# Near-key attention scores: three fp32r matmuls with split operands, or one fp32 matmul per 64x32 tile

## The chip, the cores and the metric

One core of a Trainium2 chip runs the whole program. The metric is device time in microseconds (us) of one execution, lower is better. All data are fp32 in memory; "fp32r" is the type under which TensorE reads an fp32 word at reduced precision in one pass, and "fp32" the type under which one matmul stands in the trace as two records of the same shape, two passes.

## What is computed

Two layers of a decoder, for a prompt of 1024 tokens and a sample group of 32 tokens. Layer 0 projects the normalised input to seven parts, runs a causal depthwise convolution of width 31 on one branch and attention on the other, and projects both back. Layer 1 is a gated linear recurrence. The change lies in the attention of the prompt in layer 0. There are 16 heads of width 64, and each query sees three sets of keys:

```python
DSWA_CONFIGS = ((128, 1), (512, 4), (2048, 16))   # (window, dilation)
scores = einsum('ndbqhe,ndbkhe->ndbhqk', qb, kk) * (hd ** -0.5)   # per config, by stride
lse = logsumexp(scores, axis=-1)
o = einsum('ndbhqk,ndbkhe->ndbqhe', exp(scores - lse), vv)
...
w = softmax(lses, axis=0)                          # merge of the three configs
yb = einsum('cnth,cnthe->nthe', w, outs)
```

The kernel folds the three sets into one softmax: a key that is in m of the sets has weight m, which a mask adds to the score. A query needs all keys of its own and the previous 128-token block ("near"), and further back only those at a distance that is a multiple of 4 ("far").

## The kernel before

**Work of layer 0.** Feature rows are on the 128 partitions, tokens along the free axis. Every projection is a "dense" job: 128 output features, three token chunks of 384, 384 and 288 (`CW`), and for each chunk 24 fp32r matmuls (8 slices of the contraction, three products of high and low parts each) into one PSUM tile (`d`, or `x` where a bank is spare). For head pair 0 to 7 the jobs are `ag`, `av` (the convolution's gate and value), `v`, `k`, `q`; then come the 8 `g` and the 8 `ao` jobs (gates), then the output projection. When the last `av` chunk of pair p is done, `conv_thread` (L1215) is spawned: 26 taps on DVE as multiply-adds of 128x1024, 5 taps as ACT products added on POOL, a join, and a store to DRAM (`yd`). When the last `q` chunk is done, `attention` (L995) is spawned. After the attention of a pair `dec_thread` (L1432) does the sample group, with 16 loads of cached keys and values (`kc`, `vc`) for each pair.

**Rotation.** `ev_q` and `ev_k` (L843, L866) evacuate a chunk of q or k: `rope` (L813) multiplies by cosines on DVE, swaps halves on ACT, multiplies by sines on POOL and adds on DVE. q is written in class order (`by_class`): in each block of 128 tokens the 32 tokens with position = r mod 4 stand together, for r = 0 to 3. Two more steps follow in the chain of every chunk, `hi` and `lo`: `hi` writes the fp32r copy of each head's half on ACT (2 casts of 64 partitions for q, 4 for k), and `lo` the difference to the fp32 value on DVE (2 subtractions of 64 partitions). `st` holds q's high part of a head in that head's 64 partitions and its low part in the other 64; `kk` holds k's high part in both halves; `kl` holds k's low part. These are 5 pages of 1056 columns beside `q` and `k`.

**Attention of a block.** `qk(i)` (L1003) makes the scores of block i (128 queries, two heads). Near keys: `nn` = 256 columns (128 for block 0), as two matmuls per head, `st` with `kk` over all 128 partitions (high and low part of q times high part of k at once), and then q's high part with `kl` over 64 partitions. Far keys: `nf` = 32 i columns for i of 2 or more, in fp32, as 8 tiles of 64 rows by 32 columns of the array, one per class r and head h; the keys of class r are read with a stride of 4 (`r:128 * i:4`). Then DVE adds the mask and takes the row minimum (`tensor_tensor_reduce`, shown as CUSTOM_DVE_ANT_0), and ACT takes the exponential. `tr(i)` (L1038) transposes the near part in blocks of 128 on TensorE, `far(i)` (L1055) the far part in blocks of 128 or 64 columns (`FAR`: (first block, end, group, width)), DVE or ACT copies the transposes to SBUF, and `pv(i)` and `far_pv` multiply by the values.

**What sets the order.** Every engine's order is written at build time by a planner (`Kern`, L177) that keeps a clock for each engine and models every instruction's cost (`array`, L239, for TensorE; `cost`, L266, for the others). Dense matmuls are laid down in a fixed order; between them `sides` (L402) places steps of the threads (Atoms) whose inputs are ready by the model, by priority: the rotation 0, the v transposes 1, attention 2, decode 3, the convolution 5. A DVE step is placed only while DVE's clock is less than 800 ns (`QUEUE`) ahead of TensorE's. A step of attention on TensorE needs inputs that were ready 300 ns ago by the model (`LEAD`). Buffers are pages of SBUF: a job or thread starts when the pages that it claims are free (`claim`; 28 pages in all). The planner's idea of a tile's time is one line of `array`:

```python
one = max(0.4167 * n + 5 if fast else 0.8333 * n + 5, ld)
```

Of the kernel before, what the change touches and what calls it, by code (L numbers as in the profile page):

```python
# [176 lines left out]
class Kern:  # L177
# [61 lines left out]
    def array(self, s, name, a, k):  # L239
# [11 lines left out]
        if mode == (128, 128):  # L251
            d = max(0.4375 * n + 8, 107) if fast else 109 if name == "transpose" else 2 * max(0.8333 * n + 4, 111)
            free, f = s + d, s + d + 165
        else:
            p = k.get("tile_position") or (a[1].base_partition() if hasattr(a[1], "base_partition") else 0,
                                            a[0].base_partition() if hasattr(a[0], "base_partition") else 0)
            s = max(s, self.tiles.get(p, 0.0))
            ld = m / 1.2 + 20
            one = max(0.4167 * n + 5 if fast else 0.8333 * n + 5, ld)
            r = 1 if fast else 2  # L260
            self.tiles[p] = s + r * one
            free, f = s + 7 * r, s + ld + r * one + 165
# [580 lines left out]
    def ev_q(self, pr, c, p):  # L843
        nc, A = self.nc, self.A
        S = self.pair[pr]
        w = CW[c]
        if c == 0:
            S["st"] = (A.alloc(T, True), A.alloc(T, True))
            S["q"] = A.alloc(NTOK)
        cs = slice(C0[c], min(C0[c] + w, T))  # L850
        half = [(slice(64 * h, 64 * h + 64), slice(64 - 64 * h, 128 - 64 * h)) for h in range(2)]
        q = S["q"]

        def hi():
            for h, (a, b) in enumerate(half):
                nc.scalar.copy(S["st"][h].r[a, cs], q[a, cs])

        def lo():
            for h, (a, b) in enumerate(half):
                nc.vector.tensor_tensor(S["st"][h].r[b, cs], q[a, cs], S["st"][h][a, cs], op=OP.subtract)  # L860
            if c == 2:
                nc.gpsimd.tensor_copy(self.qs[:, pr * NS:pr * NS + NS], q[:, T:NTOK])

        self.rope(p, c, "rq", pr, q, [Atom(hi, "act"), Atom(lo, "dve")])

    def ev_k(self, pr, c, p):  # L866
        nc, A = self.nc, self.A
        S = self.pair[pr]
        w = CW[c]
        if c == 0:  # L870
            S["kk"] = (A.alloc(T, True), A.alloc(T, True))
            S["kl"] = A.alloc(T, True)
            S["k"] = A.alloc(NTOK)
        cs = slice(C0[c], min(C0[c] + w, T))
        half = [(slice(64 * h, 64 * h + 64), slice(64 - 64 * h, 128 - 64 * h)) for h in range(2)]
        k = S["k"]

        def hi():
            for h, (a, b) in enumerate(half):
                nc.scalar.copy(S["kk"][h].r[a, cs], k[a, cs])  # L880
            for h, (a, b) in enumerate(half):
                nc.scalar.copy(S["kk"][h].r[b, cs], S["kk"][h][a, cs])

        def lo():
            for h, (a, b) in enumerate(half):
                nc.vector.tensor_tensor(S["kl"].r[a, cs], k[a, cs], S["kk"][h][a, cs], op=OP.subtract)
            if c == 2:
                nc.gpsimd.tensor_copy(self.ks[:, pr * NS:pr * NS + NS], k[:, T:NTOK])

        self.rope(p, c, "rk", pr, k, [Atom(hi, "act"), Atom(lo, "dve")])  # L890
# [104 lines left out]
    def attention(self, pr):  # L995
# [7 lines left out]
        def qk(i):  # L1003
            def f():
# [5 lines left out]
                qc, kc = slice(128 * i, 128 * i + 128), slice(128 * (i + 1) - nn, 128 * (i + 1))  # L1010
                hs = [slice(64 * h, 64 * h + 64) for h in range(2)]
                ss = []
                for h in range(2):
                    P[i, h] = A.alloc(W + 8)
                    ss.append(self.px())
                    nc.tensor.matmul(ss[h][:, nf:W], S["st"][h].r[:, qc], S["kk"][h].r[:, kc], start=True, stop=False)
                for h in range(2):
                    nc.tensor.matmul(ss[h][:, nf:W], S["st"][h].r[hs[h], qc], S["kl"].r[hs[h], kc],
                                     start=False, stop=True)
                if nf:  # L1020
                    for r in range(4):
                        for h in range(2):
                            nc.tensor.matmul(ss[h][32 * r:32 * r + 32, 0:nf],
                                             S["q"][hs[h], 128 * i + 32 * r:128 * i + 32 * r + 32],
                                             S["k"][hs[h], r:128 * i:4], start=True, stop=True,
                                             skip_group_check=True, tile_position=(64 * h, 32 * r))
# [28 lines left out]
        def far(i):  # L1055
            def f():
                p = self.px()
                parts = [n for n, (t0, t1, g, m) in enumerate(FAR) if t0 <= i < t1]
                for n, x in enumerate(parts):
                    g, m = FAR[x][2:]  # L1060
                    for h in range(2):
                        a = 256 * n + 128 * h
                        nc.tensor.transpose(p[0:m, a:a + 128], P[i, h][:, 128 * g:128 * g + m], self.ident)
# [68 lines left out]
        def fin1():  # L1132
# [8 lines left out]
            for n in ("st", "kk"):  # L1141
                for b in S[n]:
                    b.free()
            for n in ("q", "k", "kl", "vt", "vf"):
                S[n].free()
# [1193 lines left out]
    def plan_jobs(self):  # L2339
# [17 lines left out]
        for p in range(NPAIR):  # L2357
            J["v", p] = job("v", 5, p, self.ev_v, 1, 0)
            J["g", p] = job("g", 6, p, self.ev_g, 1, 1, self.gate_thread)
            J["k", p] = job("k", 4, p, self.ev_k, 4, 4)  # L2360
            J["q", p] = job("q", 3, p, self.ev_q, 3, 4, self.attention)
# [292 lines left out]
```

## Time and profile before

| | |
|---|---|
| time, median of 3 runs | 2397.56 us (2393.16 to 2400.98) |
| the profiled execution's own time | 2401.23 us, of which the instructions span 2399.4 us |
| busy, of the span | PE 95%, DVE 71%, ACT 46%, POOL 44% |
| granted TensorE clock, mean | 0.984 of 2.4 GHz |
| chain of waits that ended last | PE 70%, DVE 18%, ACT 3%, issue 3%, DMA 3%, POOL 2% |
| moved by DMA | 271.52 MB, mean 113 GB/s |

The profile is one execution. "Busy" of TensorE (PE) is the union of its matmuls' intervals; matmuls are pipelined, so their mean durations are longer than the distance between them. PEld is the loading of the stationary operand, which runs beside PE. Tiles are called by their pools: `d`, `x` and `o` are PSUM tiles, `b` and `c` SBUF buffers. A form such as 64*32 64x224 is 64 rows by 32 columns of the array with 224 columns streamed. The helper through which all engines are called makes L157 the line of every instruction, so forms and tiles tell them apart. In order of time: layer 0's jobs with attention up to about 750 us, decode attention and the gate jobs to about 1100, the output projection to about 1300, and layer 1 after that.

### The profile page before, as it was taken

What the parts mean: (1) busy time and instruction counts of PE and PEld (TensorE: products, weight loads), DVE (VectorE), ACT (ScalarE), POOL (GpSimd) and SP (SyncE); (2) the same over time, 40 slices, a digit from 0 to 9 for tenths busy, and PEclk for the clock granted to TensorE, in tenths of its full rate; (3) what the DMA queues carried; (4) which work ended last, traced back from release to release, by engine and by line L of the source; (5) the groups of instructions that cost most, each with busy time, mean ns of one, the idle gap of its engine ahead of it and who ended that gap; (6) DMA issues with size and microseconds to landing.
All of it is one profiled execution on the core that took longest, in us unless ns stands there. A gap on an engine that the chain in (4) does not pass through costs nothing.

```text
span 2399.4 us, 41471 instructions
## 1 busy us (share of the span) xinstructions
PE 2277.0 (95%) x16619; PEld 2141.0 (89%) x16619; DVE 1700.2 (71%) x2567; ACT 1094.7 (46%) x2000; POOL 1047.6 (44%) x700
## 2 busy tenths in 40 slices
PE   7989999989999999999988999999999999999997
PEld 7977977978879877889988999999999999998996
DVE  7999989999998766654486666656666666667336
ACT  5554554544645343334345444444444444444432
POOL 6653743634645253344464333333323333335436
PEclk9999999999999999999999999999999999999998
DMA  4221221221222798875351111211111112232525
GB/s 152 62 72 41 72 70 29 83 76 39 74 83 98 256 348 334 310 282 179 107 188 61 64 63 64 69 68 63 63 66 63 64 63 73 76 108 92 180 99 174
DMA packets 118169, 271.52 MB, mean 113 GB/s; under 512 B 32336, under 2 KB 59472, under 8 KB 117968
## 3 DMA queue, kind: packets, MB, share of 16 engines
q1 hardware_dynamic: 117968, 268.78, 32.7%
q8 instruction: 133, 2.18, 0.4%
q14 instruction: 68, 0.56, 0.1%
HBM read 215.00 MB, written 53.73 MB: 112 GB/s over the span
## 4 chain that ended last, share of the span: by engine, by line
PE 70%; DVE 18%; ACT 3%; issue 3%; DMA 3%; POOL 2%; SPq 0%; DVEq 0%; ACTq 0%; POOLq 0%
PE d L157 41%; PE x L157 29%; DVE b L157 18%; ACT b L157 3%; POOL b L157 2%; DMA b<-vc 1%; PE o L157 1%; DVE c L157 1%; DMA b<-x 1%; DMA b<-kc 0%; DMA ybd<-b 0%; DMA b<-rd 0%; SPq L157 0%; DMA b<-x1d 0%; DMA cpo<-b 0%
## 5 line engine op out<-in xcount | busy, mean ns | idle before, releaser
L157 PE MATMUL d<-c,b 128*128 128x384 f32 (+1 forms) x8064 | 1410.7, 330 | 18.3 <-ACT b L157 7.8
L157 PEld LDWEIGHTS d<-c,b 128*128 128x128 f32 x8064 | 1317.7, 190 | 49.8 <-issue 23.1
L157 POOL TENSOR_TENSOR b<-b,b 128x1024 f32<-128x1024 f32 (+8 forms) x418 | 834.2, 2007 | 833.7 <-ACT b L157 600.7
L157 ACT ACTIVATE b<-b 128x384 f32<-128x384 f32 (+14 forms) x647 | 357.9, 568 | 802.6 <-DVE b L157 788.5
L157 PE MATMUL x<-c,b 128*128 128x384 f32 (+4 forms) x3472 | 560.1, 311 | 30.1 <-DVE b L157 16.3
L157 PEld LDWEIGHTS x<-c,b 128*128 128x128 f32 (+2 forms) x3472 | 514.0, 174 | 57.8 <-ACT b L157 22.5
L157 DVE TENSOR_TENSOR b<-b,b 128x384 f32<-128x384 f32 (+15 forms) x397 | 405.4, 1033 | 93.3 <-ACT b L157 74.3
L157 DVE SCALAR_TENSOR_TENSOR b<-b,c,b 128x1024 f32<-128x1024 f32 (+2 forms) x258 | 387.5, 1505 | 10.9 <-ACT b L157 8.4
L157 ACT CAST b<-b 128x1024 fp32r<-128x1024 f32 (+5 forms) x408 | 293.1, 727 | 44.8 <-DVE b L157 11.4
L157 PE MATMUL x<-b,b 128*32 128x128 f32 (+11 forms) x3760 | 295.7, 329 | 6.2 <-POOL b L157 2.3
L157 DVE SCALAR_TENSOR_TENSOR b<-b,b 128x384 f32<-128x384 f32 (+3 forms) x216 | 201.5, 937 | 104.8 <-ACT b L157 104.1
L157 PEld LDWEIGHTS x<-b,b 128*32 128x32 f32 (+2 forms) x3760 | 218.6, 138 | 55.4 <-issue 27.2
L157 DVE TENSOR_TENSOR b<-d,b 128x384 f32<-128x384 f32 (+3 forms) x283 | 142.7, 511 | 147.7 <-PE d L157 140.4
L157 DVE TENSOR_TENSOR b<-x,b 128x288 f32<-128x288 f32 (+3 forms) x157 | 79.6, 507 | 127.9 <-PE x L157 112.9
L157 POOL TENSOR_SCALAR b<-b 128x32 f32<-128x32 f32 x40 | 28.8, 720 | 295.5 <-DVE b L157 295.4
L157 ACT COPY b<-x 128x512 f32<-128x512 f32 (+5 forms) x177 | 88.2, 514 | 137.6 <-PE x L157 129.8
L157 ACT COPY b<-d 32x384 f32<-32x384 f32 (+2 forms) x210 | 94.2, 448 | 106.7 <-DVE b L157 58.7
L157 DVE COPY b<-x 128x512 f32<-128x512 f32 (+6 forms) x214 | 96.0, 463 | 59.9 <-PE x L157 53.6
L157 POOL COPY b<-b 128x32 f32<-128x32 f32 (+2 forms) x105 | 56.4, 546 | 152.4 <-DVE b L157 150.2
L157 ACT ACTIVATE b<-b,c 128x512 f32<-128x512 f32 (+1 forms) x112 | 94.8, 875 | 3.0 <-DVE b L157 0.5
L157 DVE CUSTOM_DVE_ANT_0 b<-x,b 128x256 f32<-128x256 f32 (+8 forms) x144 | 71.8, 534 | 22.2 <-PE x L157 21.6
L157 PE MATMUL o<-b,b 128*64 128x128 f32 (+1 forms) x864 | 59.7, 269 | 27.4 <-DVE b L157 26.1
(59 smaller groups left out, 954.7 us busy)
## 6 DMA issues: line engine op xcount, KB each, us to landing
b<-wc SPq DMA_DIRECT2D x64, 512.0 KB, 3.8
b<-wab SPq DMA_DIRECT2D x56, 512.0 KB, 5.7
b<-kc SPq DMA_DIRECT2D x64, 448.0 KB, 6.4
b<-vc SPq DMA_DIRECT2D x64, 448.0 KB, 8.5
b<-woa SPq DMA_DIRECT2D x32, 512.0 KB, 4.6
b<-woc SPq DMA_DIRECT2D x32, 512.0 KB, 3.8
b<-yd SPq DMA_DIRECT2D x16, 528.0 KB, 8.8
ybd<-b SPq DMA_DIRECT2D x16, 512.0 KB, 3.2
```

The source lines that it names most:

```text
L157: r = f(*a, **k)
```

## The change

The near scores are no longer three products of split operands. They are computed like the far ones: fp32 `q` and `k` straight from the rotation, 8 tiles of 64x32, the near keys with unit stride, and the far keys right behind them in the same tiles. With that `hi` and `lo` go, with the pages of `st`, `kk` and `kl`: 144 casts on ACT and 96 subtractions on DVE. The far transposes always take 128 columns; of the blocks that took 64, the other 64 rows of the PSUM tile are written and not read. The planner gets a factor `u` of 2 for tiles of 64 rows that have another number of columns. The jobs `k` and `q` claim 1 page where they claimed 4 and 3.

```diff
@@ array
             ld = m / 1.2 + 20
-            one = max(0.4167 * n + 5 if fast else 0.8333 * n + 5, ld)
+            u = 2 if mode[0] == 64 != mode[1] else 1
+            one = max(0.4167 * n * u + 5 if fast else 0.8333 * n * u + 5, ld)
@@ ev_q, ev_k
-            S["st"] = (A.alloc(T, True), A.alloc(T, True))
...
-                nc.scalar.copy(S["st"][h].r[a, cs], q[a, cs])
...
-                nc.vector.tensor_tensor(S["st"][h].r[b, cs], q[a, cs], S["st"][h][a, cs], op=OP.subtract)
...
-        self.rope(p, c, "rq", pr, q, [Atom(hi, "act"), Atom(lo, "dve")])
...
+    def ev_turned(self, pr, c, p, n, smp):
         S = self.pair[pr]
         if c == 0:
+            S[n] = self.A.alloc(NTOK)
+        t = S[n]
+
+        def copy():
+            self.nc.gpsimd.tensor_copy(smp[:, pr * NS:pr * NS + NS], t[:, T:NTOK])
+
+        self.rope(p, c, "r" + n, pr, t, [Atom(copy, "pool")] if c == 2 else [])
@@ attention, qk(i)
-                    nc.tensor.matmul(ss[h][:, nf:W], S["st"][h].r[:, qc], S["kk"][h].r[:, kc], start=True, stop=False)
-                for h in range(2):
-                    nc.tensor.matmul(ss[h][:, nf:W], S["st"][h].r[hs[h], qc], S["kl"].r[hs[h], kc],
-                                     start=False, stop=True)
-                if nf:
+                q, k = S["q"], S["k"]
+                for a, b, ks in ((nf, W, kc), (0, nf, None)):
                     for r in range(4):
                         for h in range(2):
...
+                            if b > a:
+                                nc.tensor.matmul(ss[h][32 * r:32 * r + 32, a:b],
+                                                 q[hs[h], 128 * i + 32 * r:128 * i + 32 * r + 32],
+                                                 k[hs[h], ks or slice(r, 128 * i, 4)], start=True, stop=True,
+                                                 skip_group_check=True, tile_position=(64 * h, 32 * r))
@@ attention, far(i)
-                        nc.tensor.transpose(p[0:m, a:a + 128], P[i, h][:, 128 * g:128 * g + m], self.ident)
+                        nc.tensor.transpose(p[:, a:a + 128], P[i, h][:, 128 * g:128 * g + 128], self.ident)
@@ plan_jobs
-            J["k", p] = job("k", 4, p, self.ev_k, 4, 4)
-            J["q", p] = job("q", 3, p, self.ev_q, 3, 4, self.attention)
+            J["k", p] = job("k", 4, p, self.ev_k, 1, 4)
+            J["q", p] = job("q", 3, p, self.ev_q, 1, 4, self.attention)
```

The planner lays out all engines anew, so much stands in another order than before. Three places matter here.

TensorE, scores of block 3 of the first pair (`x` is the score tile; before, `b_580` and `b_581` are `kk`, `b_582` is `kl`, `b_697` and `b_698` `st`, `b_583` k and `b_699` q; the dense matmuls `d` around it are of the next pair's jobs). Before:

```order
L157 MATMUL d<-c_79,b_909 128x288
L157 MATMUL d<-c_71,b_910 128x288
L157 MATMUL x<-b_580,b_697 128x256
L157 MATMUL x<-b_581,b_698 128x256
L157 MATMUL x<-b_582,b_697 128x256
L157 MATMUL x<-b_582,b_698 128x256
L157 MATMUL x<-b_583,b_699 32x96 x8
L157 MATMUL d<-c_72,b_909 128x288
```

Now (`b_580` is k, `b_694` is q):

```order
L157 MATMUL d<-c_79,b_781 128x288
L157 MATMUL d<-c_71,b_782 128x288
L157 MATMUL x<-b_580,b_694 32x256 x8
L157 MATMUL x<-b_580,b_694 32x96 x8
L157 MATMUL d<-c_72,b_781 128x288
L157 MATMUL d<-c_80,b_781 128x288
```

Four near matmuls of the whole array became eight of one 64x32 tile each; the eight far ones stand behind them as before. Counted in dense matmuls from the program's start, the scores of block 1 of the second pair stand behind 816 of them where they stood behind 867, and those of block 7 behind 924 where they stood behind 939.

SyncE's queue in the middle of the pairs (`ko` is the store of pair 2's keys, which the attention of that pair waits for; `cpo` and `cso` follow `av` of pair 3; `yd` is the store of convolution 2's result; `rd` belongs to the end of pair 2's attention). Before:

```order
L157 DMA ko<-b_2431 128x1056
L157 DMA cpo<-b_2669 128x30
L157 DMA cso<-b_2670 1024x1x30
L157 DMA b_2917<-wab 128x1024
L157 DMA vo<-b_2925 128x1056
L157 DMA yd<-b_2284 128x1056
L157 DMA rd<-b_3297 16x128
```

Now:

```order
L157 DMA ko<-b_2434 128x1056
L157 DMA b_2828<-wab 128x1024
L157 DMA yd<-b_2158 128x1056
L157 DMA cpo<-b_2663 128x30
L157 DMA cso<-b_2664 1024x1x30
L157 DMA b_3046<-wab 128x1024
L157 DMA vo<-b_3065 128x1056
L157 DMA b_3311<-wab 128x1024
L157 DMA rd<-b_3412 16x128
```

The result of convolution 2 is stored ahead of `cpo` of pair 3 where it was stored behind `vo` of pair 3: the taps of a convolution are laid down earlier, before those of the next one can begin.

SyncE's queue where decode attention begins (`dmask` is decode's mask, `wab` weights of the gate jobs, `ybd` the attention output, `kc` cached keys). Before:

```order
L157 DMA b_7218<-dmask 128x960
L157 DMA b_7266<-wab 128x1024
L157 DMA b_7338<-ybd 128x1024
L157 DMA b_7368<-wab 128x1024
...
L157 DMA b_7876<-wab 128x1024
L157 DMA ybd<-b_7838 128x1024
L157 DMA b_8070<-ybd 128x1024
L157 DMA b_8088<-kc 128x896
```

Now:

```order
L157 DMA b_7216<-dmask 128x960
L157 DMA b_7262<-wab 128x1024
L157 DMA ybd<-b_6388 128x1024
L157 DMA b_7271<-kc 128x896
L157 DMA b_7276<-kc 128x896
```

The first load of cached keys stands behind one weight load after `dmask` where it stood behind five.

## Rows read from the trace of the kernel before

**Rows 1.** Busy time by engine in three stretches; first line names the columns.

```profile
core 0: us, PE busy (x) PEld busy (x) DVE busy (x) ACT busy (x) POOL busy (x), PEclk, DMA share, GB/s
100.00:750.00 650.00, 601.51 (x4666) 534.62 (x4665) 598.88 (x813) 331.84 (x724) 315.46 (x198) 0.98 0.21 63
750.00:1100.00 350.00, 333.82 (x3163) 287.35 (x3163) 228.68 (x405) 126.11 (x230) 134.25 (x117) 0.99 0.76 281
...
1300.00:2300.00 1000.00, 990.93 (x6632) 977.02 (x6631) 611.65 (x1032) 458.31 (x750) 370.77 (x242) 1.00 0.22 76
```

**Rows 2.** Chain of waits in 100 to 750 us, its shares by engine and tile.

```profile
by line: DVE b L157 50.5%; PE d L157 23.0%; ACT b L157 7.9%; PE x L157 7.0%; issue 6.3%; POOL b L157 2.8%; PE o L157 2.4%; DMA cpo<-b 0.2%; DVEq L157 0.0%; ACTq L157 0.0%; POOLq L157 0.0%
```

**Rows 3.** Busy time, one pair: rotation of k and q, then attention.

```profile
179.00:206.00 27.00, 26.89 (x167) 25.49 (x166) 23.39 (x41) 15.08 (x34) 9.85 (x9) 1.00 0.13 42
206.00:246.00 40.00, 34.46 (x354) 26.36 (x355) 39.01 (x61) 17.48 (x41) 14.24 (x9) 1.00 0.13 42
```

**Rows 4.** Waits of PE in 100 to 750 us: total us, times, longest.

```profile
PE o L157 <- DVE b L157: 26.1, 25, 2.8
...
PE x L157 <- DVE b L157: 10.5, 7, 2.2
PE x L157 <- ACT b L157: 10.2, 6, 3.0
```

**Rows 5.** Timeline of PE, blocks 0 and 1 of one pair: start, us, what.

```profile
377.01 0.59 PE L157 MATMUL x<-b,b 128*128 128x128 f32 x4
377.53 0.79 PE L157 MATMUL d<-c,b 128*128 128x384 f32 x3
378.15 0.71 PE L157 MATMUL x<-b,b 128*128 128x256 f32 x4
378.80 1.32 PE L157 MATMUL d<-c,b 128*128 128x384 f32 x6
```

**Rows 6.** Groups of PE by form, whole span: busy us, mean ns, idle before.

```profile
L157 PE MATMUL x<-b,b 128*32 128x128 f32 x1152 | 39.9, 282 | 3.5 <-ACT b L157 2.3 <-DVE b L157 1.2
...
L157 PE MATMUL x<-b,b 128*32 128x512 f32 x128 | 20.5, 605 | 2.4 <-POOL b L157 2.3
...
L157 PE MATMUL x<-c,b 128*64 128x128 f32 x96 | 17.1, 273 | 0.0
...
L157 PE MATMUL x<-b,b 64*32 64x224 f32 x128 | 8.0, 565 | 0.0
...
L157 PE MATMUL x<-b,b 64*32 64x64 f32 x128 | 3.5, 284 | 0.0
```

**Rows 7.** Stationary loads of v transposes, 423.94 to 424.57 us: columns with unit stride.

```profile
L157 PEld LDWEIGHTS x<-c,b 128*128 128x128 f32 x7 | 0.7, 141 | 0.1
```

**Rows 8.** The same, 424.80 to 425.15 us: columns read with a stride of 4.

```profile
L157 PEld LDWEIGHTS x<-c,b 128*128 128x128 f32 x4 | 0.6, 206 | 0.0
```

**Rows 9.** DVE's groups by form, 100 to 750 us: taps, and the subtractions.

```profile
L157 DVE SCALAR_TENSOR_TENSOR b<-b,c,b 128x1024 f32<-128x1024 f32 x171 | 274.5, 1605 | 2.3
L157 DVE TENSOR_TENSOR b<-b,b 64x384 fp32r<-64x384 f32 x58 | 49.8, 858 | 1.2
...
L157 DVE TENSOR_TENSOR b<-b,b 64x256 fp32r<-64x256 f32 x30 | 26.8, 894 | 0.5
```

**Rows 10.** ACT's casts by form, 100 to 750 us.

```profile
L157 ACT CAST b<-b 64x384 fp32r<-64x384 f32 x84 | 43.1, 513 | 1.7
...
L157 ACT CAST b<-b 64x256 fp32r<-64x256 f32 x42 | 16.9, 403 | 7.5 <-DVE b L157 6.8
```

**Rows 11.** Chain of waits in 750 to 1100 us, its shares.

```profile
by line: PE d L157 44.5%; PE x L157 20.5%; DVE b L157 9.2%; DMA b<-vc 7.3%; issue 4.5%; POOL b L157 3.5%; DMA b<-kc 2.6%; ACT b L157 2.3%; DMA ybd<-b 1.5%; DMA b<-rd 1.4%; PE o L157 1.2%; DVE c L157 1.1%; SPq L157 0.4%; ACTq L157 0.0%; DVEq
```

**Rows 12.** Timeline of SyncE's queue: end of `av` 2, store of convolution 2.

```profile
203.17 0.34 SPq L157 DMA_DIRECT2D cpo<-b  x1
...
330.42 0.33 SPq L157 DMA_DIRECT2D yd<-b  x1
```

More of the change, by code (lines that the diff above doesn't have):

```diff
@@ L843, in ev_q, with ev_k @@
     def ev_q(self, pr, c, p):
-        nc, A = self.nc, self.A
+        self.ev_turned(pr, c, p, "q", self.qs)
+    def ev_k(self, pr, c, p):
+        self.ev_turned(pr, c, p, "k", self.ks)
+    def ev_turned(self, pr, c, p, n, smp):
         S = self.pair[pr]
-        w = CW[c]
         if c == 0:
-            S["st"] = (A.alloc(T, True), A.alloc(T, True))
[L849 to L855, printed above, removed]
-                nc.scalar.copy(S["st"][h].r[a, cs], q[a, cs])
-        def lo():
-            for h, (a, b) in enumerate(half):
-                nc.vector.tensor_tensor(S["st"][h].r[b, cs], q[a, cs], S["st"][h][a, cs], op=OP.subtract)
-            if c == 2:
-                nc.gpsimd.tensor_copy(self.qs[:, pr * NS:pr * NS + NS], q[:, T:NTOK])
-        self.rope(p, c, "rq", pr, q, [Atom(hi, "act"), Atom(lo, "dve")])
[L866 to L890, printed above, removed]
+            S[n] = self.A.alloc(NTOK)
[3 more added lines that the diff above has]
+        self.rope(p, c, "r" + n, pr, t, [Atom(copy, "pool")] if c == 2 else [])
     def tok4(self, src, out, g):
@@ L1009, in f @@
                 W = nf + nn
-                qc, kc = slice(128 * i, 128 * i + 128), slice(128 * (i + 1) - nn, 128 * (i + 1))
+                kc = slice(128 * (i + 1) - nn, 128 * (i + 1))
                 hs = [slice(64 * h, 64 * h + 64) for h in range(2)]
@@ L1015, in f @@
                     ss.append(self.px())
-                    nc.tensor.matmul(ss[h][:, nf:W], S["st"][h].r[:, qc], S["kk"][h].r[:, kc], start=True, stop=False)
-                for h in range(2):
-                    nc.tensor.matmul(ss[h][:, nf:W], S["st"][h].r[hs[h], qc], S["kl"].r[hs[h], kc],
-                                     start=False, stop=True)
-                if nf:
+                q, k = S["q"], S["k"]
+                for a, b, ks in ((nf, W, kc), (0, nf, None)):
                     for r in range(4):
                         for h in range(2):
[L1023 to L1026, printed above, removed]
+                            if b > a:
[3 more added lines that the diff above has]
+                                                 skip_group_check=True, tile_position=(64 * h, 32 * r))
                 t = self.cur
@@ L1140, in fin1 @@
             den.free()
[L1141 to L1144, printed above, removed]
+            for n in ("q", "k", "vt", "vf"):
                 S[n].free()
```

## The prediction

> **What bounds the kernel now.** I read the stretches first [rows 1]. In layer 1 (1300 to 2300 us) PE is busy 990.93 of 1000 us and DVE 611.65: PE alone sets the pace, and the change touches nothing there. The stretch with the attention of the prompt, 100 to 750 us, looks otherwise: PE 601.51 and DVE 598.88 of 650 us, both at 92%. Two engines so near to full cannot be ranked by busy time, so the chain of waits of that stretch comes next [rows 2]: half of it, 50.5%, runs over DVE, 32.4% over PE (23.0, 7.0 and 2.4), 7.9% over ACT. One pair shows how these take turns [rows 3]: while k and q are rotated PE is full (26.89 of 27 us) and DVE has some room (23.39); while the blocks of attention run DVE is full (39.01 of 40) and PE has gaps (34.46). The waits name them [rows 4]: of PE's idle 48.5 us (650 less 601.51) 46.8 end with DVE or ACT, most of it (26.1) at the products with the values, which wait for a copy of the transposes that stands in DVE's queue. That queue is filled by the taps of the convolution: 171 of them at 1605 ns, 274.5 us of the stretch [rows 9]. The reader should see a stretch that both engines share, with DVE a little ahead as the bound.
>
> **PE, near scores.** Before, near scores alone take from the start of their four matmuls to the next dense one 0.65 us for a block with 256 near columns (378.15 to 378.80) and 0.52 us for block 0 with 128 (377.01 to 377.53) [rows 5]. So 128 columns cost 0.13 us and some 0.39 us do not depend on columns: the array goes through two changes of shape there, to 64x128 and on. Afterwards there is one change, and the tiles serve the far keys too; I count half, 0.2 us. The columns are then two passes of 256, and the question is the price of one column. Two prices stand in the trace [rows 6]. The far tiles of 64x32 grow from 284 to 565 ns over 160 columns, 1.76 ns a column. Decode's tiles of 128x32 grow from 282 to 605 ns over 384 columns, 0.84 ns. In both, four column tiles run side by side on different columns; what differs, beside the height of a tile, is that decode reads its keys with unit stride and the far keys have a stride of 4. The stride has a price elsewhere in the trace: the same transposes load 128 stationary columns in 141 ns with unit stride [rows 7] and in 206 ns with a stride of 4 [rows 8]. The near keys have unit stride, so I take 0.84, and keep 1.76 as the other end.
>
> At 0.84: 2 x 256 x 0.84 ns + 0.2 = 0.63 us against 0.65 for blocks 1 to 7, and 0.42 against 0.52 for block 0: 0.24 us less for a pair, 2 us less for eight. At 1.76: 1.10 and 0.65 us, so 0.45 more seven times and 0.13 once, 3.3 us for a pair and **26 us** more for eight.
>
> The Trainium skill (Advanced Engine Details and Errata, SBUF Cachelines) says that reads which stay in the same 16-byte line run at full speed and that a read in a new line each time pays a penalty; a stride of four fp32 words is such a case. The slower strided load above agrees with it. By that rule the term is the 2 us less; by the far rows taken as a price of the tile's shape, which the planner's new factor also does, it is the 26 us more.
>
> **PE, transposes.** Those 64 wide take 273 ns each [rows 6], those 128 wide the same matmul of 128 columns, and the load behind it is 141 ns at most beside the running matmul. Zero; were that cover gone, 64 of them by 30 ns would be 2 us.
>
> **DVE and ACT.** The 96 subtractions go; 88 of them lie in the stretch, 49.8 + 26.8 = 76.6 us of DVE [rows 9]. The casts in the stretch are 43.1 + 16.9 = 60 us of ACT [rows 10]. None of this lies where DVE is full: it lies in the rotation, where PE is the bound [rows 3]. It is worth something only because DVE's queue is one queue. Freed there, it takes taps that now stand between the blocks of attention, and the order shows this: the result of convolution 2 is now stored before the next convolution can begin, where at present it is stored 127 us after its own `av` [rows 12], behind the next one's. Taps that come forward also come forward into this stretch: I take the convolutions to end earlier by half of one, 13 of its 26 taps, by 1.6 us = 21 us of work that used to fall behind 750 us. So DVE loses 76.6 - 21 = 56 us in the stretch, and half of the chain there is DVE's: 56 x 0.505 = 28 us. ACT's 60 us at its share of 7.9% are 5 us. Together **33 us**. The bounds are 0 (all of it refilled) and the 48.5 us for which PE is idle.
>
> **Decode.** The first load of cached keys moves up by four weight loads. In 750 to 1100 us PE is idle 16.2 us [rows 1], and the loads of `kc` and `vc` are 9.9% of the chain [rows 11], 35 us. I take a third of the idle time, 5 us, between 0 and 16. The pages set free are what lets the loads move; what they run into is DMA already 76% busy there.
>
> **Costed at nothing.** The rotation's chain is two steps shorter, so attention begins sooner; that is how taps and blocks come apart, and is counted above. The copies of the sample rows stay on POOL. Eight weight splits move from DVE to POOL (44% busy), off both bounds.
>
> **The sum.** 2 + 33 + 5 = 40 us less. The profiled execution took 2401.23 us, so 2361; the median of the runs is 3.7 us lower, and against it I forecast **2358 us**. Layer 1 and the output projection move as a whole.
>
> **The rivals.**
> - *The tile's shape costs, not the stride.* Near columns at 1.76 ns: PE gains 26 us of work where it loses 2. DVE's relief stays at most as it was, so 28 us are added: 2386 us. For it: the far tiles are the only ones in the trace that use both halves of the array in fp32, so their price may belong to that. Against it: the fp32r tiles of 64x128, also two halves at once, let the near scores of 256 columns cost only 0.13 us more than those of 128 [rows 5], and the strided load is slow without any tiles [rows 8].
> - *The relief does not come.* The blocks wait on their own order of steps (score, mask, exponential, transpose, copy), not on DVE's throughput. Then 7 us remain of the 40: 2391 us. For it: what is removed lies in the stretch where PE is full. Against it: DVE at 39.01 of 40 us between the blocks.
> - *PE becomes the bound, slower than before.* Near columns at 1.76 ns, and the taps go on filling DVE between the blocks, so the waits stay: + 26 and nothing back, 2424 us. It decides once the dearer columns outweigh the relief: with no relief that is so from a price of about 0.9 ns a column (3.84 us a pair for each ns, against 3.47 saved), with the full 38 us from about 2.1. For it: the planner now plans these tiles at twice their length, so it hands DVE more room between blocks, which taps may fill. Against it: the same as above, twice.
>
> **How the numbers follow.** The forecast has 0.55, the dear tile with relief 0.25, no relief 0.10, the slower case 0.10. I call 0.3%, 7 us, the least that a measurement of this kernel tells from no change, so "same" is 2390 to 2405. The forecast's own range is 2330 to 2382: relief between some 10 and 48.5 us, decode 0 to 16. All of it is faster. Of the dear tile, 12 us below the median with 15 us of spread, 0.15 is faster, 0.07 the same and 0.03 slower; of no relief half is faster and half the same; the last is slower. That is 0.75, 0.12 and 0.13. The range of 8 in 10 is 2325 to 2402: it takes in the dear tile and no relief, and leaves out the slower case and the tails.
>
> **What would show it.** Right: forms 64*32 64x256 at 284 + 192 x 0.84 = about 450 ns, 896 records; DVE below 560 us busy in the matching stretch and a chain there with PE ahead of DVE; PE's waits for DVE at `o` and `x` cut by half or more; layer 0's end some 40 us sooner and layer 1 as long as now. Wrong: 64x256 near 620 ns (the tile's shape), or the same waits of PE as now with DVE still at 39 of 40 us between the blocks (no relief), or decode's loads late enough that PE waits longer than 16 us behind 750 us.

## The result, and the profile after

| | |
|---|---|
| time after, median of 4 runs | 2373.81 us (2371.72 to 2375.06) |
| time before, median of 4 runs beside it | 2395.56 us (2393.16 to 2400.98) |
| ratio, 95% interval | 0.9905 [0.9885, 0.9925] |
| forecast | 2358 us (2325 to 2402), faster |
| span of the profiled execution | 2371.2 us, 28.2 less than before |

The kernel is 21.8 us faster where 40 were forecast. The sign and the range held; about half of the forecast gain is missing. The first view is the busy time of the stretches, in the columns of [rows 1], of the kernel after.

```profile
100.00:750.00 650.00, 614.92 (x5681) 531.27 (x5679) 562.11 (x774) 289.71 (x636) 350.40 (x216) 0.99 0.26 81
750.00:1100.00 350.00, 338.76 (x3050) 300.84 (x3049) 201.20 (x362) 121.83 (x215) 127.83 (x112) 0.98 0.74 269
...
1300.00:2300.00 1000.00, 991.28 (x6597) 977.32 (x6596) 600.05 (x1008) 449.60 (x739) 370.28 (x242) 1.00 0.23 77
```

Layer 1 is as full of PE as it was, so what was gained was gained ahead of it. In 100 to 750 us PE idles 35.1 us (650 less 614.92) where it idled 48.5, and DVE is down by 36.8 us to 562.11. The chain of waits of the same stretch, and PE's waits there (engine, tile, who was waited for: total us, times, longest):

```profile
by line: PE d L157 34.7%; DVE b L157 33.8%; PE x L157 9.9%; issue 7.5%; ACT b L157 5.8%; POOL b L157 3.3%; PE o L157 3.0%; DMA b<-rd 1.3%; DMA rd<-b 0.4%; SPq L157 0.2%; DVEq L157 0.1%; POOLq L157 0.0%; ACTq L157 0.0%
```

```profile
PE x L157 <- DVE b L157: 17.2, 13, 3.1
PE o L157 <- DVE b L157: 6.0, 10, 1.2
PE o L157 <- ACT b L157: 4.4, 6, 1.7
PE x L157 <- POOL b L157: 3.8, 1, 3.8
PE x L157 <- ACT b L157: 3.5, 3, 1.7
```

Against [rows 2], DVE's share of the chain fell from 50.5% to 33.8% and PE's rose from 32.4% to 47.6 (34.7, 9.9 and 3.0). Against [rows 4], the wait of the value products for DVE is nearly gone (26.1 to 6.0 us), but waits at `x` for DVE grew (10.5 to 17.2). The stretch changed its bound, though not all the way. Groups of PE by form in it (busy us, mean ns, idle before):

```profile
L157 PE MATMUL x<-b,b 64*32 64x256 f32 x864 | 35.8, 388 | 0.0
...
L157 PE MATMUL x<-b,b 64*32 64x224 f32 x112 | 7.0, 565 | 0.0
```

The near tiles take 388 ns over 256 columns, while the far ones in the same tiles take 565 over 224, as before [rows 6]. The scores as a whole got shorter on PE. These are the scores of block 2 of the third pair and the dense matmul behind them, before and after:

```profile
299.92 1.08 PE L157 MATMUL x<-b,b 128*128 128x256 f32 x20
300.93 0.80 PE L157 MATMUL d<-c,b 128*128 128x384 f32 x3
```

```profile
272.33 0.89 PE L157 MATMUL x<-b,b 64*32 64x256 f32 x32
273.15 1.13 PE L157 MATMUL d<-c,b 128*128 128x384 f32 x5
```

From the first matmul of the scores to the next other one it is 1.01 us before and 0.82 after. Summed over all 64 blocks of the eight pairs, these stretches take 73.8 us before and 61.0 after, 12.8 us less. DVE's taps, and the two steps of SyncE's queue that answer to [rows 12]:

```profile
L157 DVE SCALAR_TENSOR_TENSOR b<-b,c,b 128x1024 f32<-128x1024 f32 x187 | 316.2, 1691 | 2.5
```

```profile
202.32 0.34 SPq L157 DMA_DIRECT2D cpo<-b  x1
...
286.42 0.33 SPq L157 DMA_DIRECT2D yd<-b  x1
```

Convolution 2 is now stored 84 us behind its `av` (127 before), and 187 taps stand in the stretch (171 before).

**Where the gain shows.** Before, dense work stops between the later blocks of a pair. These are busy times of the 20 us that hold the scores of pair 4's blocks 4 to 7 in the kernel before: all work, then the dense tiles `d` alone (the columns without POOL, which has none there).

```profile
494.50:514.50 20.00, 14.23 (x171) 8.87 (x172) 19.68 (x35) 7.61 (x19) 0.21 (x1) 1.00 0.07 28
```

```profile
494.50:514.50 20.00, 0.39 (x3) 0.15 (x2) 0.45 (x1) 0.00 (x0) 1.00 0.07 28
```

And the kernel after, the blocks of the same pair (440 to 490 us) and what follows them until the next pair's:

```profile
440.00:490.00 50.00, 48.03 (x508) 38.78 (x506) 42.36 (x71) 20.03 (x50) 20.68 (x15) 1.00 0.14 31
490.00:528.00 38.00, 34.65 (x244) 33.19 (x245) 34.16 (x32) 19.29 (x39) 28.32 (x17) 1.00 0.30 94
```

```profile
440.00:490.00 50.00, 33.35 (x178) 27.59 (x176) 4.22 (x10) 0.00 (x0) 1.00 0.14 31
490.00:528.00 38.00, 30.08 (x179) 29.25 (x180) 3.63 (x7) 10.66 (x24) 1.00 0.30 94
```

Before, PE had 0.39 us of dense work in those 20 us and stood idle for 5.8 while DVE was full. Now two thirds of the time between the blocks (33.35 of 50 us) is dense work, and PE idles 2.0 us in 50; over 50 us of the kernel before (484.50 to 534.50) it was 21.36 us of dense work and 7.5 us idle. But 3.4 us of idle time stand in the 38 us behind them, where PE had almost none while k and q were rotated [rows 3]. The blocks are spread out, too. From the scores of block 2 to those of block 7, pair 4 took 24.0 us before by the timeline of PE (484.16 to 508.20); these are the two of the kernel after, 33.6 us apart:

```profile
449.61 0.89 PE L157 MATMUL x<-b,b 64*32 64x256 f32 x32
...
483.18 1.46 PE L157 MATMUL x<-b,b 64*32 64x256 f32 x32
```

### The profile page after: what moved, and what is told of

It is laid out like the page before. It is cut to its first block, busy times and chain, and to the rows that moved or that the text cites. A ratio compares the mean times of both kernels' runs of the same rounds, so it can differ in the third digit from the quotient of the medians.

```text
span 2371.2 us, 42772 instructions
## 1 busy us (share of the span) xinstructions
PE 2267.1 (96%) x17387; PEld 2121.7 (89%) x17387; DVE 1617.8 (68%) x2466; ACT 1025.2 (43%) x1858; POOL 1055.1 (44%) x703
## 4 chain that ended last, share of the span: by engine, by line
PE 73%; DVE 15%; issue 4%; ACT 3%; POOL 2%; DMA 2%; SPq 0%; DVEq 0%; POOLq 0%; ACTq 0%
PE d L157 41%; PE x L157 31%; DVE b L157 14%; ACT b L157 3%; POOL b L157 2%; PE o L157 1%; DVE c L157 1%; ACT c L157 0%; DMA b<-yd 0%; DMA b<-ybd 0%; DMA b<-rd 0%; DMA b<-wab 0%; SPq L157 0%; DMA b<-kc 0%; POOL c L157 0%
## 5 line engine op out<-in xcount | busy, mean ns | idle before, releaser
L157 POOL TENSOR_TENSOR b<-b,b 128x1024 fp32r<-128x1024 f32 (+6 forms) x422 | 845.8, 2015 | 860.8 <-ACT b L157 675.3
L157 PE MATMUL x<-c,b 128*128 128x384 f32 (+4 forms) x3640 | 583.1, 311 | 26.2 <-DVE b L157 21.3
L157 DVE TENSOR_TENSOR b<-b,b 128x384 f32<-128x384 f32 (+14 forms) x297 | 303.4, 1035 | 89.8 <-ACT b L157 66.6
L157 PE MATMUL x<-b,b 128*32 128x128 f32 (+12 forms) x4528 | 281.9, 339 | 5.1 <-POOL b L157 4.3
L157 PEld LDWEIGHTS x<-b,b 64*32 64x32 f32 (+3 forms) x4528 | 201.1, 127 | 56.8 <-issue 39.4
L157 ACT CAST b<-b 128x1024 fp32r<-128x1024 f32 (+3 forms) x264 | 224.7, 862 | 33.2 <-DMA b<-od 8.4
L157 DVE TENSOR_TENSOR b<-x,b 128x384 f32<-128x384 f32 (+3 forms) x162 | 81.9, 506 | 134.0 <-PE x L157 119.0
L157 ACT COPY b<-x 128x512 f32<-128x512 f32 (+4 forms) x177 | 86.4, 498 | 147.7 <-PE x L157 130.1
L157 DVE COPY b<-x 128x512 f32<-128x512 f32 (+8 forms) x216 | 100.5, 476 | 71.8 <-PE x L157 60.3
L157 DVE CUSTOM_DVE_ANT_0 b<-x,b 128x128 f32<-128x128 f32 (+8 forms) x144 | 72.0, 532 | 51.9 <-PE x L157 47.7
L157 POOL TENSOR_TENSOR b<-b,c 128x248 f32<-128x248 f32 (+1 forms) x48 | 66.8, 1406 | 36.2 <-PE d L157 33.2
```

The lines of the kernel that those rows point to most:

```text
L157: r = f(*a, **k)
```

## The experiments

Twelve kernels ran, in three groups of four (e1 to e4; e6 to e9; e10 to e13, on another chip), each timed against the kernel before on the same chip (medians of before 2396.28, 2395.18 and 2396.08 us). The results, with the terms that each kernel has:

| run | near scores | casts, subtractions | planner's factor | us | ratio to before [95%] |
|---|---|---|---|---|---|
| e6 | new | both, unused | none | 2396.86 | 1.0009 [0.9999, 1.0019] |
| e1 | new | both, unused | near and far | 2414.71 | 1.0077 [1.0060, 1.0094] |
| e7 | old | both | far, and near's 64x128 | 2405.52 | 1.0041 [1.0026, 1.0056] |
| after | new | none | near and far | 2373.81 | 0.9905 [0.9885, 0.9925] |
| e3 | new | none | none | 2356.75 | 0.9834 [0.9817, 0.9850] |
| e11 | new | none, pages held | none | 2346.02 | 0.9789 [0.9773, 0.9806] |
| e12 | new | casts, unused | none | 2363.48 | 0.9864 [0.9847, 0.9880] |
| e8 | new | none | far alone | 2346.08 | 0.9802 [0.9782, 0.9821] |
| e10 | new | none | near alone | 2352.45 | 0.9815 [0.9798, 0.9833] |
| e2 | new, near keys at stride 4 | none | near and far | 2391.50 | 0.9979 [0.9969, 0.9988] |
| e4 | new, far keys at stride 1 | none | none | 2345.51 | 0.9787 [0.9771, 0.9803] |
| e9 | as e4, a tap less on DVE | none | none | 2347.39 | 0.9806 [0.9788, 0.9824] |
| e13 | new, transposes as before | none | near and far | 2377.12 | 0.9921 [0.9905, 0.9938] |

### What the relief of DVE and ACT is worth: e1, e6, e12, e11

e1 puts the casts and subtractions behind the rotation again; nothing reads them.

```diff
-        self.rope(p, c, "r" + n, pr, t, [Atom(copy, "pool")] if c == 2 else [])
+        d = S["s" + n]
...
+        def hi():
+            for h, (a, b) in enumerate(half):
+                self.nc.scalar.copy(d[h].r[a, cs], t[a, cs])
...
+        def lo():
+            for h, (a, b) in enumerate(half):
+                o = d[2].r[a, cs] if n == "k" else d[h].r[b, cs]
+                self.nc.vector.tensor_tensor(o, t[a, cs], d[h][a, cs], op=OP.subtract)
...
+        self.rope(p, c, "r" + n, pr, t, [Atom(hi, "act"), Atom(lo, "dve")])
```

> The changed kernel with the casts and subtractions that made the split copies of q and k put back (144 on ScalarE, 96 on VectorE, some 77 us and 60 us of busy time in layer 0), their result used by nothing; the scores stay in the new form. Claims of pages for jobs k and q back to 4 and 3. Theory (the gain comes mostly from the work taken off VectorE and ScalarE): 2387 to 2392 us, VectorE's busy time in 100 to 750 us back near 620 us, and PE's waits for VectorE at x and o up again. Rival (the gain comes from the shorter scores on PE; VectorE had room): 2374 to 2378 us, with the waits of the changed kernel.

2414.71 us, 40.9 above the changed kernel and above the kernel before: outside both expectations. PE's waits for DVE in 100 to 750 us came back, though DVE's busy time there is 589.69 us and not near 620:

```profile
PE o L157 <- DVE b L157: 42.7, 23, 3.4
PE x L157 <- DVE b L157: 25.1, 8, 4.5
```

The work is worth about what the whole forecast was, so something else in the change costs time. e6 is e1 with `u = 1` (the planner's factor taken out).

> As the first experiment (new scores, the casts and subtractions put back with their result unused), but without the planner's factor of two; to be read against the changed kernel without the factor, 2356.75 us. Theory (the work taken off VectorE and ScalarE is worth about 35 us, and the factor costs some 17 us beside it, each on its own): 2390 to 2400 us, about the kernel before. Rival (the relief is worth 41 us only under the factor's poor order): 2360 to 2380 us.

2396.86 us, the time of the kernel before. So new scores and wider transposes, with the old work kept and without the factor, change the time by +1.7 us, which the interval doesn't tell from zero. On PE the scores are as much shorter in e6 as in the changed kernel (61.2 us in sum, 73.8 before), but PE only waits longer, mostly for DVE: it idles 56.2 us in 100 to 750 us, 48.5 before. e11 keeps e6's pages and claims and drops the work, e12 drops the subtractions alone.

```diff
+            S["s" + n] = tuple(self.A.alloc(T, True) for _ in range(2 if n == "q" else 3))
...
-            J["k", p] = job("k", 4, p, self.ev_k, 1, 4)
+            J["k", p] = job("k", 4, p, self.ev_k, 4, 4)
```

and in e12, with `hi` as above:

```diff
+        self.rope(p, c, "r" + n, pr, t, [Atom(hi, "act")] + ([Atom(copy, "pool")] if c == 2 else []))
```

> The changed kernel without the planner's factor (2356.75 us), with the five pages of the split copies held by each pair again and claimed by jobs k and q, but nothing written into them: it takes back the pages and leaves the relief of the engines. Theory (the relief of VectorE and ScalarE is the gain): 2356 to 2364 us; the forecast's 5 us for earlier loads of cached keys would be in that. Rival (the pages set free are what the gain comes from): 2380 to 2397 us.

> As the run with the pages held, and ScalarE's 144 casts put back as well, their result unused; the 96 subtractions on VectorE stay out. Between that run and the one with casts and subtractions both (2396.86 us) it divides the relief between the two engines. Theory (VectorE's part is the larger, 28 to 5 in the forecast): some 5 us above the run with the pages held, 2360 to 2370 us. Rival (casts delay the rotation's chain, ScalarE's part is as large as VectorE's): 2375 to 2385 us.

2346.02 and 2363.48 us. e11 is 10 us below its range; e12 is within its own, though 17.5 above e11 where some 5 were expected. From e6 to e12 the subtractions are worth 33.4 us, from e12 to e11 the casts 17.5, together 50.8 with the pages held. With the pages given back, as in the change, casts and subtractions are worth 40.1 (e6 less e3). The rival of the pages is refuted: holding them made the kernel no slower, but 10.7 us faster than e3. PE's waits in 100 to 750 us of e6, of e12 and of e11:

```profile
PE o L157 <- DVE b L157: 29.8, 28, 1.7
PE x L157 <- DVE b L157: 13.8, 6, 3.8
PE x L157 <- ACT b L157: 9.6, 5, 3.9
```

```profile
PE x L157 <- DVE b L157: 19.4, 7, 4.7
PE o L157 <- DVE b L157: 7.3, 10, 2.0
PE x L157 <- ACT b L157: 3.1, 2, 2.8
```

```profile
PE x L157 <- DVE b L157: 15.6, 7, 3.4
PE o L157 <- DVE b L157: 2.7, 4, 1.2
```

The subtractions give the value products their copies sooner (29.8 to 7.3 us). The casts' part shows in smaller waits of several kinds (7.3 to 2.7, 19.4 to 15.6, 3.1 to none).

### What the planner's factor costs: e3, e8, e10, e7

e3 takes it out of the changed kernel, e8 keeps it for the far scores (stride 4), e10 for the near ones; e7 puts the line of the change into the kernel before.

```diff
-            u = 2 if mode[0] == 64 != mode[1] else 1
+            u = 1
```

```diff
-            u = 2 if mode[0] == 64 != mode[1] else 1
+            u = 2 if mode[0] == 64 != mode[1] and a[2].ap[-1][0] == 4 else 1
```

(e10 has `!= 4` there.)

> The factor of two that the planner puts on 64-row tiles of other than 64 columns is taken out; nothing else. It changes only the order and the fill. If the planner's better length of the scores is part of the gain: 5 to 10 us slower, near 2380 us. If it is not (rival; the near tiles, two thirds of the columns, run at half the planned price): 2368 to 2375 us.

2356.75 us, 17.1 below the changed kernel and 11 us below the rival's range. Busy time and PE's waits of e3, 100 to 750 us, and its chain:

```profile
100.00:750.00 650.00, 633.30 (x5867) 550.05 (x5865) 580.82 (x805) 294.69 (x644) 348.32 (x212) 0.99 0.28 86
```

```profile
PE x L157 <- DVE b L157: 10.9, 7, 2.4
PE o L157 <- DVE b L157: 3.6, 3, 1.2
PE x L157 <- ACT b L157: 1.8, 1, 1.8
PE o L157 <- ACT b L157: 0.3, 1, 0.3
```

```profile
by line: PE d L157 61.9%; PE x L157 15.2%; DVE b L157 13.3%; PE o L157 4.8%; issue 2.9%; ACT b L157 1.9%; DVEq L157 0.0%; ACTq L157 0.0%
```

PE's waits sum to 16.6 us here and to 34.9 in the changed kernel, 18.3 us apart, about the 17.1 us. The computation is the same, so it is the order, and with it which engine takes a copy. DVE is on 13.3% of the chain and PE on 81.9, and pair 4 takes 27.9 us from block 2's scores to block 7's. Note that DVE is busier than in the changed kernel (580.82 against 562.11): a kernel that gets through sooner brings more work into the same 650 us (5867 records of PE against 5681).

> The changed kernel with the factor of two kept for the far scores alone (the ones that are read with a stride of 4, and measured at 1.76 ns a column), and taken off the near ones (0.84 ns). Theory (it is the near scores, planned at twice their measured price, that cost the 17 us): 2350 to 2360 us. Rival (any longer plan costs, or orders just scatter by this much): 2364 to 2376 us.

> The kernel before with the planner's factor alone: it meets there the far scores and the 64x128 tiles of the near ones; no instruction is added or taken away, only the order moves. Theory (a length that is planned too long costs, in whatever kernel): 2403 to 2415 us. Rival (before, the far tiles' length was what was wrong, and the factor mends it): 2385 to 2398 us.

e8 came out at 2346.08 us, below its range, e7 at 2405.52, 10.3 above the kernel before as the theory had it. That read as "a length that is planned too long costs", and e10 put it to the test.

> The changed kernel with the planner's factor of two on the near scores alone and taken off the far ones: the fourth case beside both (2373.81 us), none (2356.75) and far alone (2346.08). Theory (each of the two lengths has its own cost, a wrong one in either costs, and they add): 2356.75 + 27.7 = 2380 to 2388 us, the worst of the four. Rival (orders scatter, and far alone was luck): anything from 2346 to 2376 us.

2352.45 us: **the theory fell.** The factor on the near scores alone costs nothing against e3, on the far ones alone nothing, on both 17.1 us. So the length planned for either kind of tile costs nothing by itself. Four kernels without both, e3, e8, e10 and e11, lie between 2346.0 and 2356.8 us with the same computation: orders of one and the same work scatter by 10.7 us. The changed kernel lies 17.1 above the worst of them. That this one order came out badly by chance is not excluded, but every kernel with the full factor is slower than its partner without: 17.1 us here, 17.9 with the splits' work kept (e1 less e6), 10.3 in the kernel before (e7, where the factor meets other near tiles). e13 below is one more order with the full factor, and stands at 2377.12 us. Between e1 and e6 a part can be the clock. The same view over 100 to 600 us, for e1 and then e6:

```profile
100.00:600.00 500.00, 444.62 (x3959) 391.83 (x3958) 449.07 (x623) 241.85 (x533) 238.52 (x152) 0.95 0.21 59
```

```profile
100.00:600.00 500.00, 453.38 (x4252) 397.69 (x4250) 445.24 (x636) 251.62 (x557) 229.85 (x145) 0.98 0.21 59
```

A mean granted clock of 0.95 is 10% of the stretch at 1.2 GHz, 50 us, and 0.98 is 20 us. By estimate, 30 us more at half the clock are at most 15 us of PE's work. Between the changed kernel and e3 there is no such difference (0.99 in both, 100 to 750 us).

### Stride or shape: e2, e4, e9

e2 reads the near keys as the far ones are read; e4 lets POOL write a copy of k by class, `kf`, which the far scores read with unit stride, without the factor; e9 is e4 with `PTAPS` 6 in place of 5.

```diff
-                                                 k[hs[h], ks or slice(r, 128 * i, 4)], start=True, stop=True,
+                                                 k[hs[h], slice(r, 4 * (b - a), 4) if ks else slice(r, 128 * i, 4)], start=True, stop=True,
```

```diff
+                self.nc.gpsimd.tensor_copy(S["kf"].f.rearrange("p (r a) -> p r a", r=4)[:, :, a:a + w],
+                                           t[:, C0[c]:C0[c] + 4 * w].rearrange("p (a r) -> p r a", r=4))
...
-                                                 k[hs[h], ks or slice(r, 128 * i, 4)], start=True, stop=True,
+                                                 (k[hs[h], ks] if ks else S["kf"][hs[h], 256 * r:256 * r + b]), start=True, stop=True,
```

> The near scores read every fourth column of k, as the far scores do, in place of neighbouring ones; so the keys are other ones than the reference's, number and form of the matmuls are the same. If the stride sets the price of a column (1.76 against 0.84 ns): the 64x256 matmuls go from 388 to about 620 ns, a pair of heads' scores get some 3.5 us longer, and the kernel comes out at 2390 to 2402 us. If the shape of the tile sets it (rival): 388 ns and 2374 us stay.

2391.50 us, 17.7 above the changed kernel, as expected if the stride sets the price. The scores on PE, summed as above, take 88.4 us, 27.4 more than in the changed kernel, so with the relief there most of their time counts. Forms of e2, then of e4, 100 to 750 us:

```profile
L157 PE MATMUL x<-b,b 64*32 64x256 f32 x816 | 57.0, 623 | 0.0
```

```profile
L157 PE MATMUL x<-b,b 64*32 64x256 f32 x880 | 36.5, 388 | 0.0
...
L157 PE MATMUL x<-b,b 64*32 64x224 f32 x128 | 4.7, 349 | 0.0
...
L157 PE MATMUL x<-b,b 64*32 64x64 f32 x128 | 2.5, 216 | 0.0
```

> POOL writes a copy of each pair's k in which the columns stand by class (every fourth together), 24 copies of 128x256 or so more on POOL, and the far scores read it with stride one; without the planner's factor. If the stride sets the price: 64x224 matmuls from 564 to some 355 ns, PE's busy time in 100 to 750 us down by some 10 to 20 us, and the kernel at 2360 to 2370 us if PE's path counts there, 2372 to 2376 us if VectorE still sets the pace between the blocks (then PE's waits for it rise by what PE saves). If the shape sets the price: 564 ns stay, and POOL's copies make it 0 to 5 us slower.

The stride sets the price, both ways: the same 64x256 tiles go from 388 to 623 ns with stride 4, the same 64x224 tiles from 565 to 349 ns with stride 1. At stride 1 a column costs (349 - 216) / 160 = 0.83 ns, beside 1.76 at stride 4 [rows 6]. That is a factor of 2.1 for a moving operand (the keys that stream through the array). The Trainium skill (Advanced Engine Details and Errata, SBUF Cachelines) has the direction, a penalty for a new 16-byte line at each access, and these runs agree (388 against 623 ns). e4 took 2345.51 us, better than any of its expectations, with 48.0 us of scores on PE. But its 11.2 us against e3 are no more than about what orders scatter, and e8 and e11 reach the same time with strided far keys. So whether the shorter far tiles made it faster stays open.

> The kernel with the far keys copied by class and without the factor (2345.51 us), with one more tap of each convolution moved from VectorE to ScalarE and POOL (some 1.6 us of VectorE per convolution and half, 13 us in layer 0). Theory (PE now bounds the stretch, with VectorE behind it on the chain): 2342 to 2350 us, no change. Rival (VectorE still bounds the blocks): 2330 to 2340 us.

2347.39 us, no change, as the theory said: with one tap in 26 less on DVE no gain is seen once PE leads the stretch, though one smaller than the scatter of orders would not show.

### The transposes: e13

```diff
-                        nc.tensor.transpose(p[:, a:a + 128], P[i, h][:, 128 * g:128 * g + 128], self.ident)
+                        nc.tensor.transpose(p[0:m, a:a + 128], P[i, h][:, 128 * g:128 * g + m], self.ident)
```

> The changed kernel with the transposes of the far probabilities 64 or 128 wide again, as in the kernel before. The forecast counted the wider ones at nothing: 2371 to 2377 us. Rival (the 64-wide ones force a change of the array's shape, and planner and array each gain by their going): 2378 to 2390 us.

2377.12 us, 3.3 above the changed kernel and between the two expectations, with intervals of the two ratios that overlap. No cost of the wider transposes is seen, and no gain beyond the scatter.

**Versions that beat both kernels.** All seven that have neither the subtractions nor the full factor (e3, e4 and e8 to e12). The fastest are e4, e11 and e8 at 2345.51 to 2346.08 us, a ratio of 0.979 to 0.980 to the kernel before. The runs don't tell the three apart. e8 is the changed kernel with one condition more in the planner.

## Why the prediction was right in sign and half in size

The measured chain from the kernel before to the changed one: + 1.7 us for the new scores and transposes with the splits' work and pages kept (e6), + 17.9 for the planner's factor on top (e1), - 40.9 for the work and pages taken away (after): - 21.3, against 21.8 measured directly. By the other way round it is + 1.7 (e6), - 40.1 for the work and pages (e3), + 17.1 for the factor (after). Such chains add up by the way they are made. What they do show is that the relief is worth the same with the factor and without it.

- *Near scores, -2 us: the price right, the size wrong.* The price of a column goes by its stride, as the sum took it. 388 ns is even less than the some 450 forecast, because the 284 ns that this started from [rows 6] were those of a strided tile; at stride 1 the 64x64 tile takes 216. But the scores got 12.8 us shorter on PE. The sum took the part that doesn't depend on columns from blocks 0 and 1, which have no far tiles; where far tiles follow, as in block 2, 0.19 us go and not 0.02. In the kernel's time none of it shows in e6, where PE waits for DVE instead. With the relief there, longer scores do cost (e2), so a part of the gain that is booked to the relief below may be these scores, which the relief lets count. How much was not measured. The rival of the tile's shape is refuted by e2 and e4; its 26 us of dearer columns are the 27.4 of e2.
- *DVE and ACT, -33 us: right in kind, and about in size.* Measured 40.9 under the changed kernel's factor and 40.1 without it, 50.8 with the pages held. Of the 50.8, DVE's part is 33.4 where "56 x 0.505 = 28 us" stood and ACT's is 17.5 where "ACT's 60 us at its share of 7.9% are 5 us" stood; each of the parts carries the scatter of single orders, 10.7 us, so that only the casts come out dearer than forecast by more than that, and by little. A share of the chain is not a bound of what an engine's work costs. One reason may be that the casts stand ahead of what DVE and PE wait for; that was argued, not shown. The upper bound of 48.5 us was passed with the pages held, by less than the scatter.
- *How the relief works: only in part as told.* Taps did come forward, 16 where 13 were assumed, at 1691 ns where 1605 were, so DVE's taps in the stretch grew by 41.7 us, not 21, and its busy time fell by 36.8, not 56. The gain went another way: dense passes moved in between the blocks, where PE had next to none in the later ones, and the blocks spread out over more time (33.6 us for 24.0). Of the text's marks, PE came out ahead of DVE on the chain, but PE's waits for DVE at `o` and `x` fell from 36.6 to 23.2 us, not by half (14.5 in e3). The end of layer 0 came 26 us sooner, not 40, by one store at the end of the output projection (`spo`, at 1327.38 and 1301.21 us). "DVE below 560 us" missed by 2 us, and by e3's 580.82 us it was no good mark.
- *Decode, -5 us: met in number, its reason not supported.* PE idles 11.2 us in 750 to 1100 us where it idled 16.2, and the first load of cached keys moved from 792.64 to 701.34 us. But with the pages held (e11) it comes at 758.08 us, and the kernel is 10.7 us faster than e3, which loads first at 667.91. SyncE's queue, after and e11, then the stretch from 750 to 1100 us of e3 and of e11:

```profile
701.34 1.76 SPq L157 DMA_DIRECT2D b<-kc  x3
```

```profile
758.08 2.24 SPq L157 DMA_DIRECT2D b<-kc  x4
```

```profile
750.00:1100.00 350.00, 335.20 (x2966) 298.34 (x2965) 193.20 (x343) 119.07 (x203) 143.99 (x116) 0.98 0.72 263
```

```profile
750.00:1100.00 350.00, 342.79 (x3136) 306.03 (x3135) 198.78 (x363) 125.69 (x221) 135.16 (x120) 1.00 0.77 282
```

PE idles 14.8 us there in e3 and 7.2 in e11, which loads 90 us later; so an earlier start of the loads alone does not shorten PE's waits.

- *The planner's factor: this is the step that failed.* The sum had no term for it. It stands in the text only under the rival in which PE becomes the bound: "the planner now plans these tiles at twice their length, so it hands DVE more room between blocks, which taps may fill". That was tied to a price of 1.76 ns, which the loss doesn't need, and its mechanism is not shown: PE's waits for DVE are longer with the line (23.2 us at `o` and `x`, 14.5 in e3), but e8 and e10 plan one kind of tile at twice its length and lose nothing. The order with both costs 17.1 us (after less e3), and that is nearly the missing 18. Without the line, e3 is 39.5 us below before, where 40 were forecast. With orders that scatter by 10.7 us, so close an agreement is partly luck.
- *The rivals.* "The relief does not come" is refuted by e1, e6 and e11. "PE becomes the bound, slower than before" is what e1 looks like in time (+ 18.4), but for another reason: there DVE keeps its work under the factor's order.

**What stays open.** Why the order with both factors loses 17 us and those with one of them none. The trace shows where: PE's waits for DVE, ACT and POOL, twice as long in sum, spread over blocks and rotations. Which rule of the planner makes it was not tried. Nor was the clock's part in e1 separated, nor that of the shorter scores from that of the relief.

## What to carry to other kernels

Work on an engine that is not the bound at that moment (casts and subtractions in a rotation where PE is the bound) can be worth a good part of its length (here 40 to 51 us for 137 us on two engines), if that engine's queue is later the one that others wait for; leave it out and look for the gain as work that moves elsewhere. Shorter work on the engine that waits may show nothing until then (e6). When a change also alters the lengths by which an order is planned, that is a change of its own: measure it apart, and first find out how far orders of the same work scatter (here 10.7 us in 2350), before a single order's gain or loss is given a cause. Plan a column of a moving fp32 operand that is read with a stride of four words at twice the price (1.76 against 0.83 ns in tiles of 64x32); other strides and tiles were not tried.

## What the runs showed that was not expected

- Four orders of the same arithmetic lie 10.7 us apart (2346.0 to 2356.8 us), more than the runs of one order (some 4 to 8 us from lowest to highest).
- Holding five pages for nothing and loading decode's keys 90 us later (758.08 against 667.91 us in e3) cost no time.
- The price of 2.1 times for a moving operand with stride 4 holds per column; at 64 columns, where not all of the time goes by columns, 284 ns [rows 6] stand against 216.
- New scores that are 12.6 us shorter on PE than the old ones gained nothing where PE waited for DVE instead (e6).
- The granted clock differs between orders of the same work: over 100 to 600 us it is 0.95 in e1, where PE idles 55.4 us, and 0.98 in e6 with 46.6. But PE's idle time alone doesn't set it: the changed kernel has 1.00 with 23.5 us, e4 0.98 with 17.6.
